# VectorE's first column sum for a pair of combined weights is queued behind the third remainder of the pair in front

## The chip, the cores and the metric

One core of one Trainium2 chip runs the whole program. The metric is the device time of one execution in microseconds, smaller is better; the median of three executions is given, and one further execution was recorded by the profiler. PE is TensorE's matmul, PEld its weight load, DVE is VectorE, ACT is ScalarE, POOL is GpSimd, SP issues DMAs.

## The reference

One layer of a hybrid trunk on 2048 frames of width 1024, in float32:

```python
h = rmsnorm(x, norm_mix_w)
u_b, u_c, u_h, z, xbc, dt_raw = split(h @ w_in)          # 1024 x 5648
y_a = short_conv_mixer(u_b, u_c, u_h, short_conv_w)       # u_b * conv3(u_c * u_h)
y_b = ssd_mixer(z, xbc, dt_raw, ...)                      # conv4, chunked state-space scan, gate, group norm
x = x + concat(y_a, y_b) @ w_out                          # 2048 x 1024
h = rmsnorm(x, norm_mlp_w)
x = x + square(relu(h @ w_up)) @ w_down                   # 1024 x 4096 and back
return rmsnorm(x, final_norm_w)
```

## The kernel before

Each float32 operand of a large matmul is split into two float32r parts: a high part `hi` (a cast on ACT, line 100 for weights) and the remainder `lo = raw - hi` (a subtraction on DVE, line 101). A product is then three matmuls, hi·hi, hi·lo and lo·hi (lines 296 to 298).

The input projection, the up projection and the down projection multiply 2x2 blocks with seven block products instead of eight (class `Seven`). Frames are taken in halves of 1024, a half being two blocks of 512 columns. Weights come in pairs of raw tiles r0 and r1, up to 1024 columns each, with a left half a and a right half b. `combine` makes of them four weight tiles in the order in which the products use them: r0 itself, s12, s34 and the right half of r1. The sums are, by halves of their tiles: s12a = r1a + r1b (line 252, which I call the first column sum), s12b = s12a - r0a, s34a = r0a - r1a, s34b = r0b - s12b (line 229 all three). Each of the four is split by `split_w`, so that a pair of weights has four casts and four remainders; the third remainder is that of s34.

`chain` runs the seven products of a pair in the order b11, t1, t2, b21, t3, b22, t4 with the accumulators px, py, px, pw, px, py, px: the three further products on px and the one on py add to what stands in the bank already. So what t2 left in px has to be copied out before t3's first matmul, and what t3 left before t4's. In the projections and the down projection one product is twelve matmuls of 512 columns. While pair n is multiplied, `chain` asks the generator `ahead` for the weights of pair n + 1: the loads after b11, the first two splits after b21, the third after b22, the fourth after t4.

This is the order in which the program is written down. A scheduler then orders each engine's instructions by written priority and by when it reckons that their inputs and buffers are there, so that an instruction can be moved far ahead of the place where it is written. Each engine executes its own list in that order; an instruction whose wait has not ended holds everything behind it on its engine. `tc.issue_after(ins)` gives the instructions of its block an edge without a semaphore: the scheduler may not put them ahead of `ins` on the same engine.

Buffers: raw tiles `wraw` have three, hi and lo four each, the sums `s` two. With three raw tiles, r0 and r1 of pair n + 1 and r0 of pair n + 2 are held at once; r1 of pair n + 2 takes the buffer that r0 of pair n + 1 leaves when its remainder is done.

`combine` runs for the first half of the input projection (20 pairs), the first half of the up projection (16) and all of the down projection (33). In the second halves of the two projections the sums are read back from memory (`pairs`, lines 323 to 325; stored at lines 255 and 261), with no sum on DVE. t3's evictions are on DVE, at line 776 in the input projection, 926 in the up projection and 1109 in the down projection. The work of the norm for the next half (lines 396 to 417, `lx` and `nb`) and the casts and remainders of the next activations (lines 368 and 369) run beside the products.

Of the kernel before, what the change touches and what calls it, by code (L numbers as in the profile page):

```python
# [11 lines left out]
F32 = mybir.dt.float32  # L12
F32R = mybir.dt.float32r
AF = mybir.ActivationFunctionType
ALU = mybir.AluOpType
# [25 lines left out]
def trunk(ctx: ExitStack, tc: tile.TileContext, x, w_in, w_dt, w_out, w_up, w_down, cvec, hrow, out):  # L41
    nc = tc.nc
# [37 lines left out]
        out=tri, in_=tri, compare_op=ALU.is_ge, fill=0.0, base=0, pattern=[[1, P]], channel_multiplier=-1  # L80
# [7 lines left out]
    def wtile(w=1024):  # L88
        hi = wp.tile([P, 1024], F32R, tag="whi", name="whi", bufs=4)[:, 0:w]
        lo = wp.tile([P, 1024], F32R, tag="wlo", name="wlo", bufs=4)[:, 0:w]  # L90
        return hi, lo
# [6 lines left out]
    def split_w(raw, eng):  # L98
        hi, lo = wtile(raw.shape[-1])
        nc.scalar.copy(hi, raw)  # L100
        eng.tensor_tensor(out=lo, in0=raw, in1=hi.bitcast(F32), op=ALU.subtract)  # L101
        return hi, lo

    def split_src(src):
        k = src.shape[1]
        return [t.rearrange("p (k c) -> p k c", k=k) for t in split_w(load_w(src), nc.vector)]
# [104 lines left out]
    class Seven:  # L211
# [35 lines left out]
        def combine(self, r0, r1, kept=None):  # L247
            w = r0.shape[-1] // 2
            a, b = slice(0, w), slice(w, 2 * w)
            yield split_w(r0, nc.vector)  # L250
            s12 = self.sumtile("s12")[:, 0 : 2 * w]
            nc.vector.tensor_tensor(out=s12[:, a], in0=r1[:, a], in1=r1[:, b], op=ALU.add)
            self.sub(s12[:, b], s12[:, a], r0[:, a])
            if kept is not None:
                nc.sync.dma_start(kept[:, 0], s12)
            yield split_w(s12, nc.vector)
            s34 = self.sumtile("s34")[:, 0 : 2 * w]
            self.sub(s34[:, a], r0[:, a], r1[:, a])
            self.sub(s34[:, b], r0[:, b], s12[:, b])
            if kept is not None:  # L260
                nc.sync.dma_start(kept[:, 1], s34)
            yield split_w(s34, nc.vector)
            yield split_w(r1[:, b], nc.vector)

        def chain(self, groups, ws, ahead, evict, after):
# [1476 lines left out]
```

## Time and profile before

| | us |
|---|---|
| median of three executions (2623.39 to 2628.8) | 2623.73 |
| the profiled execution | 2627.32 |
| its span, first to last instruction | 2625.6 |
| PE busy in the span | 2601.6 |
| DVE busy | 1917.3 |
| ACT busy | 1468.0 |

The profiled execution is 3.6 us longer than the median of the three, and its time holds 1.7 us around the span. Granted TensorE clock: 0.997 of full speed. Stages in the span: the start up to 85 us, first half of the input projection to 470, its second half with the first half of the scan to 940, output projection with the rest of the scan to 1372, up projection first half to 1655 and second half to 1985, down projection to 2590, tail.

How to read the lines: the timeline gives start, duration, engine, source line, operation, tiles, shape, count, and in brackets the idle time of the engine before the instruction with what ended it. A list of waits gives who waited for whom: total us, times, longest.

### The profile page before, as it was taken

The numbers are of one execution on the slowest core, as the hardware profiler recorded it, in microseconds if no ns is written. First come the engines' busy times: TensorE is split into PE (matmuls) and PEld (weight loads), VectorE is DVE, ScalarE is ACT, GpSimd is POOL, SyncE is SP. The second block draws the span as 40 slices with busy tenths as digits, with TensorE's granted clock in tenths as the row PEclk, the third lists the DMA queues.
The fourth block names the chain that finished last, engine by engine and source line by source line (L and its number), as shares of the span: only waits on it lengthen the run. The fifth ranks groups of instructions, "written<-read, shape, count | busy, mean of one in ns | idle before, by whom it ended". The sixth has DMA issues, their size and how long they took to land.

```text
span 2625.6 us, 33818 instructions
## 1 busy us (share of the span) xinstructions
PE 2601.6 (99%) x12139; PEld 2141.9 (82%) x12139; DVE 1917.3 (73%) x2631; ACT 1468.0 (56%) x2230; POOL 58.1 (2%) x99
## 2 busy tenths in 40 slices
PE   9999999999999999999999999999999999999998
PEld 7788888788888888888888888888888888888887
DVE  7877877777778777778677775744448887888985
ACT  7654345776667666768335555755556444444533
POOL 1010000000000000000000000000000000000001
PEclk9999999999999999999999999999999999999998
DMA  4545745644555578877656786765557654665762
GB/s 155 194 172 181 278 143 194 208 156 164 170 165 173 167 270 257 272 221 230 206 196 237 263 314 235 280 212 193 197 192 254 194 174 153 217 200 180 244 201 69
DMA packets 252169, 536.98 MB, mean 205 GB/s; under 512 B 26208, under 2 KB 93024, under 8 KB 252000
## 3 DMA queue, kind: packets, MB, share of 16 engines
q1 hardware_dynamic: 251856, 534.29, 61.1%
q8 instruction: 95, 1.56, 0.2%
q14 instruction: 74, 0.61, 0.1%
q10 hardware_dynamic: 144, 0.52, 0.1%
HBM read 354.89 MB, written 179.83 MB: 204 GB/s over the span
## 4 chain that ended last, share of the span: by engine, by line
PE 86%; DMA 5%; DVE 4%; ACT 3%; issue 2%; SPq 0%; POOL 0%; POOLq 0%; DVEq 0%; ACTq 0%
PE px L296 13%; PE px L297 13%; PE px L298 13%; PE py L296 6%; PE py L298 6%; PE py L297 6%; PE pm L113 4%; PE pm L114 4%; PE pm L115 4%; PE pw L296 3%; PE pw L298 3%; PE pw L297 3%; PE yd L1391 1%; PE yo L1388 1%; DMA ry<-yn_d 1%
## 5 line engine op out<-in xcount | busy, mean ns | idle before, releaser
L296 PE MATMUL px<-uh,whi 128*128 128x512 f32 x1672 | 655.7, 392 | 6.7 <-DVE res L1109 1.9
L298 PE MATMUL px<-uh,wlo 128*128 128x512 f32 x1672 | 651.4, 390 | 0.0
L297 PE MATMUL px<-ul,whi 128*128 128x512 f32 x1672 | 650.9, 389 | 0.0
L296 PEld LDWEIGHTS px<-uh,whi 128*128 128x128 f32 x1672 | 313.9, 188 | 80.8 <-DVE acc L1109 3.1
L101 DVE TENSOR_TENSOR wlo<-wraw,whi 128x512 fp32r<-128x512 f32 (+1 forms) x213 | 221.1, 1038 | 211.9 <-ACT whi L100 209.7
L298 PEld LDWEIGHTS px<-uh,wlo 128*128 128x128 f32 x1672 | 313.8, 188 | 66.0 <-issue 0.2
L297 PEld LDWEIGHTS px<-ul,whi 128*128 128x128 f32 x1672 | 314.0, 188 | 64.0
L100 ACT CAST whi<-wraw 128x1024 fp32r<-128x1024 f32 x214 | 193.9, 906 | 305.4 <-PE px L297 228.0
L100 ACT CAST whi<-s 128x1024 fp32r<-128x1024 f32 x210 | 219.9, 1047 | 228.4 <-PE py L297 95.0
L296 PE MATMUL py<-uh,whi 128*128 128x512 f32 x836 | 327.2, 391 | 1.3 <-ACT s L773 0.8
L298 PE MATMUL py<-uh,wlo 128*128 128x512 f32 x836 | 325.5, 389 | 0.0
L297 PE MATMUL py<-ul,whi 128*128 128x512 f32 x836 | 325.5, 389 | 0.0
L101 DVE TENSOR_TENSOR wlo<-s,whi 128x1024 fp32r<-128x1024 f32 x210 | 255.1, 1215 | 71.5 <-ACT whi L100 69.4
L113 PE MATMUL pm<-uh,whi 128*128 128x512 f32 (+1 forms) x648 | 251.6, 389 | 0.1
L114 PE MATMUL pm<-ul,whi 128*128 128x512 f32 (+1 forms) x648 | 248.2, 383 | 0.5 <-DVE ul L226 0.5
L115 PE MATMUL pm<-uh,wlo 128*128 128x512 f32 (+1 forms) x648 | 248.2, 383 | 0.0
L296 PEld LDWEIGHTS py<-uh,whi 128*128 128x128 f32 x836 | 156.9, 188 | 35.9 <-ACT s L773 1.3
L298 PEld LDWEIGHTS py<-uh,wlo 128*128 128x128 f32 x836 | 156.9, 188 | 32.7
L297 PEld LDWEIGHTS py<-ul,whi 128*128 128x128 f32 x836 | 157.0, 188 | 32.1
L368 ACT CAST uh<-rh 128x1024 fp32r<-128x1024 f32 (+1 forms) x128 | 120.4, 944 | 78.0 <-PE py L298 61.7
L296 PE MATMUL pw<-uh,whi 128*128 128x512 f32 x418 | 163.4, 391 | 0.0
L298 PE MATMUL pw<-uh,wlo 128*128 128x512 f32 x418 | 162.8, 389 | 0.0
(259 smaller groups left out, 3799.8 us busy)
## 6 DMA issues: line engine op xcount, KB each, us to landing
hid_d<-e SPq DMA_DIRECT2D x96, 512.0 KB, 3.9
rh<-hid_d SPq DMA_DIRECT2D x96, 512.0 KB, 4.3
wraw<-w_in SPq DMA_DIRECT2D x68, 512.0 KB, 3.9
wraw<-w_down SPq DMA_DIRECT2D x104, 256.0 KB, 3.7
wraw<-w_up SPq DMA_DIRECT2D x48, 512.0 KB, 4.1
dec<-rd_d SPq DMA_DIRECT2D x32, 512.0 KB, 5.7
wraw<-w_out SPq DMA_DIRECT2D x32, 512.0 KB, 5.0
x_d<-xt SPq DMA_DIRECT2D x64, 256.0 KB, 3.9
```

The costliest lines, as they stand in the source:

```text
L100: nc.scalar.copy(hi, raw)
L101: eng.tensor_tensor(out=lo, in0=raw, in1=hi.bitcast(F32), op=ALU.subtract)
L113: nc.tensor.matmul(out, whi, hi, start=(k == 0), stop=False)
L114: nc.tensor.matmul(out, whi, lo, start=False, stop=False)
L115: nc.tensor.matmul(out, wlo, hi, start=False, stop=(k == nk - 1))
L296: nc.tensor.matmul(p, hi, h[0], start=not seeded and k == 0, stop=False, **kw)
L297: nc.tensor.matmul(p, hi, h[1], start=False, stop=False, **kw)
L298: nc.tensor.matmul(p, lo, h[0], start=False, stop=(k == len(g) - 1), **kw)
L368: nc.scalar.copy(p[i][0], t)
L1388: nc.tensor.matmul(yo[:, j * L : (j + 1) * L], state[:, j * P : (j + 1) * P], cT, start=True, stop=True)
L1391: nc.tensor.matmul(yd[(i % 2) * 64 : (i % 2) * 64 + 64, (i // 2) * L : (i // 2 + 1) * L], byhead(t["xdt"])[:, i, :], t["dec"][:, i % 2 * 4 ...
```

## The change

From its second call on, `combine` writes its first column sum under `issue_after` of the third remainder of the pair whose weights were combined before. No instruction is added or removed.

```diff
     def split_w(raw, eng):
         hi, lo = wtile(raw.shape[-1])
         nc.scalar.copy(hi, raw)
-        eng.tensor_tensor(out=lo, in0=raw, in1=hi.bitcast(F32), op=ALU.subtract)
+        split["last"] = eng.tensor_tensor(out=lo, in0=raw, in1=hi.bitcast(F32), op=ALU.subtract)
         return hi, lo
+
+    split = {}
...
             s12 = self.sumtile("s12")[:, 0 : 2 * w]
-            nc.vector.tensor_tensor(out=s12[:, a], in0=r1[:, a], in1=r1[:, b], op=ALU.add)
+            cut = split.get("third")
+            with tc.issue_after(cut.ins) if cut else nullcontext():
+                nc.vector.tensor_tensor(out=s12[:, a], in0=r1[:, a], in1=r1[:, b], op=ALU.add)
...
-            yield split_w(s34, nc.vector)
+            parts = split_w(s34, nc.vector)
+            split["third"] = split["last"]
+            yield parts
             yield split_w(r1[:, b], nc.vector)
```

The order of instructions on DVE at two places. In these rows `s` is a tile of sums with its number, `wraw` a raw weight, `whi` and `wlo` its parts; line 252 of before is line 256 after, 229 is 231, 1109 is 1115, 369 is 375, 184 is 186, 776 is 782, 750 is 756.

A step of the down projection (at 2350 to 2361 us of the span), DVE before:

```order
L101 TENSOR_TENSOR wlo<-wraw,whi 128x1024
L369 TENSOR_TENSOR ul_19901<-rh,uh_19900 128x1024
L1109 TENSOR_TENSOR res<-pw,res 128x512
L101 TENSOR_TENSOR wlo<-s_19893,whi 128x1024
L252 TENSOR_TENSOR s_20039<-wraw 128x512
L1109 TENSOR_TENSOR res<-px,res 128x512
L229 TENSOR_TENSOR s_20039<-s_20039,wraw 128x512
L369 TENSOR_TENSOR ul_19940<-rh,uh_19939 128x1024
L1109 TENSOR_TENSOR acc<-py,acc 128x512
L101 TENSOR_TENSOR wlo<-s_19932,whi 128x1024
L369 TENSOR_TENSOR ul_19963<-rh,uh_19962 128x512
L229 TENSOR_TENSOR s_20078<-wraw 128x512
```

The same place after:

```order
L101 TENSOR_TENSOR wlo<-wraw,whi 128x1024
L375 TENSOR_TENSOR ul_19901<-rh,uh_19900 128x1024
L1115 TENSOR_TENSOR res<-pw,res 128x512
L101 TENSOR_TENSOR wlo<-s_19893,whi 128x1024
L1115 TENSOR_TENSOR res<-px,res 128x512
L375 TENSOR_TENSOR ul_19940<-rh,uh_19939 128x1024
L1115 TENSOR_TENSOR acc<-py,acc 128x512
L101 TENSOR_TENSOR wlo<-s_19932,whi 128x1024
L375 TENSOR_TENSOR ul_19963<-rh,uh_19962 128x512
L256 TENSOR_TENSOR s_20039<-wraw 128x512
L1115 TENSOR_TENSOR acc<-px,acc 128x512
L101 TENSOR_TENSOR wlo<-wraw,whi 128x512
```

The sum of the pair after the next (s_20039) stood ahead of t3's eviction `res<-px`; it now stands behind the third remainder (of s_19932), ahead of t4's eviction. Its three followers of line 229 come behind the fourth remainder.

A pair of the first half of the input projection (at 220 to 232 us), DVE before:

```order
L101 TENSOR_TENSOR wlo<-s_1925,whi 128x1024
L252 TENSOR_TENSOR s_2071<-wraw 128x512
L184 RECIPROCAL facc<-facc 128x512
L776 TENSOR_TENSOR eb<-px,s_1892 128x512
L776 TENSOR_TENSOR ea<-py,s_1906 128x512
L750 TENSOR_TENSOR eb<-eb,cc 128x512
L750 TENSOR_TENSOR ea<-ea,cc 128x512
L101 TENSOR_TENSOR wlo<-s_1967,whi 128x1024
L750 TENSOR_TENSOR eb<-px,cc 128x512
```

and after:

```order
L101 TENSOR_TENSOR wlo<-s_1925,whi 128x1024
L186 RECIPROCAL facc<-facc 128x512
L782 TENSOR_TENSOR eb<-px,s_1892 128x512
L782 TENSOR_TENSOR ea<-py,s_1906 128x512
L756 TENSOR_TENSOR eb<-eb,cc 128x512
L756 TENSOR_TENSOR ea<-ea,cc 128x512
L101 TENSOR_TENSOR wlo<-s_1967,whi 128x1024
L256 TENSOR_TENSOR s_2071<-wraw 128x512
L756 TENSOR_TENSOR eb<-px,cc 128x512
```

The sum left the place ahead of the norm's reciprocal and of t3's eviction `eb<-px`, and stands right ahead of t4's.

The scheduler's order of other engines moved too, in a few places. On ACT, at the second pair of the up projection (1393 to 1401 us), before:

```order
L929 ACTIVATE e_12162<-px 128x512
L100 CAST whi<-wraw 128x512
L930 ACTIVATE e_12162<-e_12162 128x512
L396 ACTIVATE lx<-lx 128x1024
L923 COPY s_12334<-px 128x512
L923 COPY s_12358<-py 128x512
L100 CAST whi<-wraw 128x1024
```

and after:

```order
L935 ACTIVATE e_12162<-px 128x512
L100 CAST whi<-wraw 128x512
L936 ACTIVATE e_12162<-e_12162 128x512
L929 COPY s_12334<-px 128x512
L929 COPY s_12358<-py 128x512
L100 CAST whi<-wraw 128x1024
```

The square of a loaded tile of the norm (`lx`) left the place ahead of the copies that empty px and py; it now stands one pair later. Its load on SP, which was issued between the stores of the two sums, now comes behind the next two weight loads.

## The prediction

> **What bounds the kernel now.** I read the page's busy times first, then busy times by stage, then who waits for what on DVE, then the timeline around each place where PE paused.
>
> ```profile
> PE 2601.6 (99%) x12139; PEld 2141.9 (82%) x12139; DVE 1917.3 (73%) x2631; ACT 1468.0 (56%) x2230; POOL 58.1 (2%) x99
> ```
>
> PE has 24.0 us of idle time in a span of 2625.6. Only that, and what a matmul that starts late loses besides, is there to win. By stage (columns: length, then busy us of PE, PEld, DVE, ACT, POOL, clock, DMA share, GB/s):
>
> ```profile
> 85.00:470.00 385.00, 382.95 (x1687) 315.42 (x1686) 292.58 (x352) 184.97 (x232) 25.49 (x40) 1.00 0.55 194
> 1372.00:1655.00 283.00, 281.98 (x1243) 232.85 (x1242) 193.32 (x256) 156.09 (x230) 0.00 (x0) 1.00 0.72 258
> 1655.00:1985.00 330.00, 330.00 (x1457) 272.92 (x1456) 169.35 (x199) 193.62 (x283) 0.00 (x0) 1.00 0.62 218
> 1985.00:2590.00 605.00, 601.97 (x2644) 494.68 (x2643) 491.81 (x630) 271.10 (x329) 0.00 (x0) 1.00 0.59 190
> ```
>
> The first, second and fourth rows are the stages that make sums on DVE; PE idles 2.05 + 1.02 + 3.03 = 6.1 us in them. In the third, the second half of the up projection, the sums are read back, and by its row PE does not idle at all: the same products without the sums run without a pause. So the sums, or what stands around them, are a suspect. On DVE:
>
> ```profile
> DVE s L252 <- DMA wraw<-w_down: 26.5, 19, 3.6
> ...
> DVE s L252 <- DMA wraw<-w_in: 11.4, 13, 1.8
> ...
> DVE s L252 <- DMA wraw<-w_up: 9.7, 9, 2.4
> ```
>
> The first column sum (line 252) waits for the load of r1 in 41 of its 69 executions, 47.6 us in all. DVE is not the bound, so this is harmless in itself. It hurts where t3's eviction stands behind it: t4's matmuls go to the same bank, and only b22's twelve matmuls, 12 x 0.23 = 2.7 us (the pitch is read below), cover that eviction.
>
> **The change, part by part.** The edit moves 68 of the 69 sums (the first has no pair in front); two of these, the first of the up and of the down projection, have a third remainder far in front and stay. The other 66 go behind it, past t3's eviction and mostly b22's. With each go the difference s12b of line 229, the store of s12 on SP in the 36 pairs that store it, and in part the two sums of s34. No duration changes. So the sum consists of pauses of PE.
>
> *First term, the worst step of the down projection:*
>
> ```profile
> 2351.14 2.33 SPq L1010 DMA_DIRECT2D wraw<-w_down  x2
> ...
> 2356.53 0.39 PE L297 MATMUL py<-ul,whi 128*128 128x512 f32 x1
> ...
> 2356.63 0.69 DVE L252 TENSOR_TENSOR s<-wraw 128x512 f32<-128x512 f32 x1 [2.65 <-DMA wraw<-w_down]
> 2356.76 0.39 PE L298 MATMUL py<-uh,wlo 128*128 128x512 f32 x1
> ...
> 2357.24 0.68 DVE L1109 TENSOR_TENSOR res<-px,res 128x512 f32<-128x512 f32 x1
> ...
> 2357.97 0.50 PE L296 MATMUL px<-uh,whi 128*128 128x512 f32 x1 [0.83 <-DVE res L1109]
> ```
>
> PE's matmuls follow each other by 0.23 us (2356.53 to 2356.76). The next starts 1.21 after its predecessor, 0.98 late, and takes 0.50 instead of 0.39, which delays its successor by another 0.11: 1.1 us. It waited for t3's eviction, whose input was there when b22 began, twelve matmuls before 2357.0, at 2354.3, and which stood behind the sum. With the sum gone DVE, idle for 2.65 us here, evicts at once and is done by 2355.0, 2 us before t4. All 1.1 us go. Two more of the kind:
>
> ```profile
> 2183.53 0.69 DVE L252 TENSOR_TENSOR s<-wraw 128x512 f32<-128x512 f32 x1 [2.29 <-DMA wraw<-w_down]
> ...
> 2184.02 0.39 PE L298 MATMUL py<-uh,wlo 128*128 128x512 f32 x1
> 2184.88 0.50 PE L296 MATMUL px<-uh,whi 128*128 128x512 f32 x1 [0.47 <-DVE acc L1109]
> ...
> 2414.75 0.69 DVE L252 TENSOR_TENSOR s<-wraw 128x512 f32<-128x512 f32 x1 [2.20 <-DMA wraw<-w_down]
> ...
> 2415.33 0.39 PE L298 MATMUL py<-uh,wlo 128*128 128x512 f32 x1
> 2416.09 0.50 PE L296 MATMUL px<-uh,whi 128*128 128x512 f32 x1 [0.38 <-DVE acc L1109]
> ```
>
> 0.86 - 0.23 + 0.11 = 0.75, and 0.76 - 0.23 + 0.11 = 0.65. Down projection: 1.1 + 0.75 + 0.65 = 2.5 us.
>
> *Second term, the input projection:*
>
> ```profile
> 222.14 0.69 ACT L183 ACTIVATE facc<-pss,cv 128x512 f32<-128x512 f32 x1
> ...
> 223.85 0.69 DVE L252 TENSOR_TENSOR s<-wraw 128x512 f32<-128x512 f32 x1 [1.76 <-DMA wraw<-w_in]
> 224.46 3.34 DVE L184 RECIPROCAL facc<-facc 128x512 f32<-128x512 f32 x1
> ...
> 227.08 0.39 PE L296 MATMUL px<-uh,whi 128*128 128x512 f32 x1
> 227.72 0.63 DVE L776 TENSOR_TENSOR eb<-px,s 128x512 f32<-128x512 f32 x1
> ...
> 228.40 0.50 PE L296 MATMUL px<-uh,whi 128*128 128x512 f32 x1 [0.93 <-DVE eb L776]
> ```
>
> The sum holds up the reciprocal, and this the eviction. PE loses 1.32 - 0.23 + 0.11 = 1.2 us. Without it the reciprocal starts when its input is there, 222.83, ends its turn 3.26 later (224.46 to 227.72), and the eviction ends at 222.83 + 3.26 + 0.63 = 226.7, ahead of 227.3. I count 1.1, since the new order of PE comes to that product two matmuls earlier.
>
> *Third term, the up projection.* Here the gain is not the sum's own:
>
> ```profile
> 1396.21 0.63 ACT L930 ACTIVATE e<-e 128x512 f32<-128x512 f32 x1
> 1398.46 1.06 ACT L396 ACTIVATE lx<-lx 128x1024 f32<-128x1024 f32 x1 [1.62 <-DMA lx<-x_d]
> ...
> 1398.71 0.39 PE L298 MATMUL pw<-uh,wlo 128*128 128x512 f32 x1
> ...
> 1399.42 0.57 ACT L923 COPY s<-px 128x512 f32<-128x512 f32 x1
> ...
> 1400.04 0.50 PE L296 MATMUL px<-uh,whi 128*128 128x512 f32 x1 [0.94 <-ACT s L923]
> ```
>
> ACT's copy of px stands behind a square that waits for a load; PE loses 1.33 - 0.23 + 0.11 = 1.2. In the new order the copy follows the instruction of 1396.21 and ends near 1397.4. The square goes one pair on, its load behind weight loads. If it waited there as long, it would cost up to 1.2 again; I take nothing, since it then stands behind the third cast, some 10 us later.
>
> *What stays or is added.* The sum with its 0.69 now stands ahead of t4's eviction or the fourth remainder; it waits there only if r1 has not landed. Four pairs of the input projection get the next pair's first cast ahead of the second SiLU and of the copy of px after t2:
>
> ```profile
> 333.04 1.06 ACT L734 ACTIVATE cacc<-cacc 128x1024 f32<-128x1024 f32 x1 [1.46 <-DVE cacc L731]
> 333.05 0.39 PE L296 MATMUL pw<-uh,whi 128*128 128x512 f32 x1
> ...
> 334.00 0.57 ACT L773 COPY s<-px 128x512 f32<-128x512 f32 x1
> 334.47 1.05 ACT L100 CAST whi<-wraw 128x1024 fp32r<-128x1024 f32 x1
> ...
> 335.77 0.39 PE L296 MATMUL px<-uh,whi 128*128 128x512 f32 x1
> ```
>
> The cast can start when t2 has ended, 333.05; then cast, SiLU and copy take 0.95 + 0.96 + 0.57 (starts to starts, the copy whole) and end at 335.5, while t3 starts at 335.77. They fit by 0.2 to 0.3 us, so 0 us; late by that, each of the four costs 0.1 to 1.2. The stores of s12 go later on SP, behind up to two weight loads; their readers are a half away, so nothing.
>
> Sum: 2.5 + 1.1 + 1.2 = 4.8 us. I give back 0.1 for the tight places: 4.7. In the profiled execution, 2627.32, that is 2622.6; its 3.6 us over the median I take to stay out of it, so 2623.73 - 4.7 = 2619.0, or -0.18%. A measurement of this kernel tells about 0.2%, 5.2 us, from no change.
>
> **The rivals.**
>
> *More goes than the named pauses* (2614.5 to 2618). Idle time in the three stages is 6.1 us by the rows, and each pause costs some 0.27 more than its idle row says (1.1 against 0.83). With a dozen pauses that is 6.1 + 12 x 0.27 = 9.3, the floor at 2614.4. For it: shorter pauses of the same kind exist. Against: part of them belong to the casts of the next activations, which stay. Some 6.5 us, 2617.
>
> *The wait only moves.* The load of r1 still starts only when r0's remainder has left the buffer:
>
> ```profile
> DMA to landing us min/median/max: 3.1/4.2/8.2
> ```
>
> In the step at 2356 the sum's new place comes after the third remainder, about 3 us after the landing seen. If the loads take near 8.2 there, DVE waits again, now ahead of t4's eviction, and half of the gain is lost: 2621.4. With the median landing it does not. The Trainium skill, "Perfetto Trace Analysis", section "Optimization Strategy", says that a bubble that repeats can mean that there is not enough SBUF for the next tile; by that rule a fourth raw tile would be the cure and a new order would not, and the time would stay at 2623.7. The rows agree that the buffer sets the load's start, not that the sum must be where it was.
>
> *The tight casts* on ACT miss in all four pairs at 1.2 each: 4.7 - 4.7, 2623.7. It decides from a conv chain on DVE 0.3 us late.
>
> *t4's eviction is late, slower.* In the pairs of the input projection whose t4 DVE evicts, twelve, the bank is needed by the next pair's t1:
>
> ```profile
> 363.79 0.69 DVE L229 TENSOR_TENSOR s<-wraw 128x512 f32<-128x512 f32 x1
> ...
> 364.40 0.68 DVE L750 TENSOR_TENSOR ch<-px,cc 128x512 f32<-128x512 f32 x1
> ...
> 365.69 0.39 PE L296 MATMUL py<-uh,whi 128*128 128x512 f32 x1
> ```
>
> The eviction ends at 365.08, 0.6 ahead of need, with one sum of 0.61 ahead of it already. Where the moved sum comes on top, up to 0.61 + 0.11 are added to PE: 12 x 0.72 = 8.6, net 3.9 slower, 2627.6; with a wait in the sum more. It decides when the third remainder ends 0.6 us later than here. Against: this pair's remainder was itself delayed by the waiting sum.
>
> **How the numbers follow.** The forecast, 2618.0 to 2619.9, 0.57, of which a third lies beyond 5.2 us; more goes 0.17; the wait moves 0.11; tight casts 0.10; late eviction 0.05, half of it over 2629 with a wait in the sum. Faster by over 0.2%: 0.17 + 0.2 = 0.37. Slower: 0.03. Within: 0.60. The range leaves out the lowest tail of the second case and the last two in part: 2615.2 to 2623.6.
>
> **What would show it.** Right: the waits of line 256 for loads fall from 47.6 us to under 10; PE's pauses at 228, 1400, 2184, 2357 and 2416 are gone; PE idles under 3 us in the three stages. Wrong: PE waits for `ch` or `eb` of line 756 at the start of a py product, for `s` of line 779 (the copy of px) in the conv pairs, or the load wait stands at line 256 as before. The prediction fails if the pauses of this one profile are not those of most executions.

## The result and the profile after

The changed kernel takes 2618.51 us (median of nine executions, 2615.68 to 2620.42) against 2623.73 of nine of the kernel before: ratio 0.9976, 95% interval 0.9967 to 0.9984, that is -5.2 us. Two later comparisons, on two chips, gave 0.9977 (0.9969 to 0.9986) and 0.9984 (0.9975 to 0.9993). All three intervals lie below 1, and the gain, about 0.2%, is about the least that a measurement of this kernel can tell. The profiled execution took 2618.51 us, its span 2616.6; the one of before had 2625.6, so the two traces differ by 9.0 us, more than the medians do.

The page's busy times, and busy times by stage (length, then PE, PEld, DVE, ACT, POOL, clock, DMA share, GB/s):

```profile
PE 2597.3 (99%) x12139; PEld 2142.4 (82%) x12139; DVE 1916.0 (73%) x2631; ACT 1468.1 (56%) x2230; POOL 61.2 (2%) x99
```

```profile
85.00:470.00 385.00, 383.39 (x1689) 315.91 (x1688) 292.12 (x352) 184.94 (x233) 29.57 (x40) 1.00 0.54 195
1372.00:1655.00 283.00, 283.00 (x1250) 234.43 (x1249) 191.92 (x256) 155.94 (x231) 0.00 (x0) 1.00 0.72 259
1655.00:1985.00 330.00, 329.83 (x1454) 272.23 (x1453) 171.34 (x201) 194.56 (x284) 0.00 (x0) 1.00 0.63 220
1985.00:2590.00 605.00, 603.19 (x2682) 498.75 (x2681) 492.65 (x632) 271.04 (x331) 0.00 (x0) 1.00 0.59 188
```

No engine does other work than before. PE's idle time falls from 24.0 to 19.3 us, in the three stages with sums on DVE from 6.1 to 1.61 + 0 + 1.81 = 3.4; in the up projection's first half it is zero. The moved instruction by itself (its line, and what DVE waited for ahead of it):

```profile
L256 DVE TENSOR_TENSOR s<-wraw x69: 421/684/693, 31.9 to 2529.3; 128x512 f32<-128x512 f32 x68, 128x256 f32<-128x256 f32 x1
its engine sat idle before it (us, times) until:
  DMA wraw<-w_down: 0.8, 1
```

47.6 us of waits in 41 sums have become 0.8 in one: at its new place r1 has landed. The step of the down projection that was the worst, in the timeline:

```profile
2349.79 0.69 DVE L1115 TENSOR_TENSOR res<-px,res 128x512 f32<-128x512 f32 x1 [0.48 <-PE px L304]
...
2352.08 0.39 PE L304 MATMUL py<-uh,wlo 128*128 128x512 f32 x1
2352.31 0.39 PE L302 MATMUL px<-uh,whi 128*128 128x512 f32 x1
...
2355.16 0.68 DVE L256 TENSOR_TENSOR s<-wraw 128x512 f32<-128x512 f32 x1
2355.76 0.68 DVE L1115 TENSOR_TENSOR acc<-px,acc 128x512 f32<-128x512 f32 x1
```

t3's eviction runs as soon as t3 ends and is done 1.8 us ahead of t4's first matmul, which follows its predecessor at the usual 0.23. The sum comes 5.4 us after that eviction, and t4's eviction is held up by nothing but the sum's 0.6 us. The pair of the input projection:

```profile
223.36 3.35 DVE L186 RECIPROCAL facc<-facc 128x512 f32<-128x512 f32 x1 [0.78 <-ACT facc L185]
...
226.63 0.63 DVE L782 TENSOR_TENSOR eb<-px,s 128x512 f32<-128x512 f32 x1
...
227.12 0.39 PE L303 MATMUL px<-ul,whi 128*128 128x512 f32 x1
...
227.35 0.46 PE L302 MATMUL px<-uh,whi 128*128 128x512 f32 x1
```

Here almost nothing is left over: the eviction ends at 227.26 and PE starts at 227.35, on time. And ACT in the up projection, where the copy of px now follows at once:

```profile
1393.85 0.63 ACT L936 ACTIVATE e<-e 128x512 f32<-128x512 f32 x1
1394.38 0.57 ACT L929 COPY s<-px 128x512 f32<-128x512 f32 x1
```

Two places are new. Once, at 288.7, the rival with the late eviction of t4 did occur:

```profile
287.85 0.68 DVE L256 TENSOR_TENSOR s<-wraw 128x512 f32<-128x512 f32 x1
...
288.45 0.68 DVE L756 TENSOR_TENSOR ch<-px,cc 128x512 f32<-128x512 f32 x1
...
289.28 0.47 PE L302 MATMUL py<-uh,whi 128*128 128x512 f32 x1 [0.19 <-DVE ch L756]
```

It cost 0.35 + 0.08 us, in this profile alone of the seven that I have with that order of the input projection. And late in the down projection DVE waits for a cast of ACT, and ACT for a load of `rh`, ahead of an eviction, this time of t2:

```profile
2515.50 1.05 ACT L374 CAST uh<-rh 128x1024 fp32r<-128x1024 f32 x1 [3.52 <-DMA rh<-hid_d]
...
2516.58 1.23 DVE L375 TENSOR_TENSOR ul<-rh,uh 128x1024 fp32r<-128x1024 f32 x1 [2.03 <-ACT uh L374]
...
2518.33 0.68 DVE L231 TENSOR_TENSOR s<-s,wraw 128x512 f32<-128x512 f32 x1
2518.93 0.69 DVE L231 TENSOR_TENSOR s<-wraw 128x512 f32<-128x512 f32 x1
2519.53 0.68 DVE L231 TENSOR_TENSOR s<-wraw,s 128x512 f32<-128x512 f32 x1
2520.13 0.68 DVE L1115 TENSOR_TENSOR acc<-px,acc 128x512 f32<-128x512 f32 x1
...
2520.87 0.50 PE L302 MATMUL px<-uh,whi 128*128 128x512 f32 x1 [1.34 <-DVE acc L1115]
```

The three sums of line 231 are the moved sum's followers; they take 1.8 us between the remainder and the eviction. Before, only two of them stood there, and PE did not pause at this place; it had paused for 1.3 us a step earlier, at 2512.

**A measure for the stages.** To compare many profiles I add up, in each stretch, by how much matmuls of 512 columns start later than 0.227 us after their predecessor, where that is more than 0.025 (late matmuls, in us). It takes in idle time and the slower first matmul behind a pause. The whole execution has 34.1 us of it before and 27.0 after; the 85 us at the start have about 6 of it in every profile.

### The profile page after: what moved, and what is told of

The parts are those of the page before. It is cut to its first block, busy times and chain, and to the rows that moved or that the text cites. A ratio compares the mean times of both kernels' runs of the same rounds, so it can differ in the third digit from the quotient of the medians.

```text
span 2616.6 us, 33846 instructions
## 1 busy us (share of the span) xinstructions
PE 2597.3 (99%) x12139; PEld 2142.4 (82%) x12139; DVE 1916.0 (73%) x2631; ACT 1468.1 (56%) x2230; POOL 61.2 (2%) x99
## 3 DMA queue, kind: packets, MB, share of 16 engines
q8 instruction: 95, 1.56, 0.2%
## 4 chain that ended last, share of the span: by engine, by line
PE 89%; DMA 4%; DVE 3%; ACT 2%; issue 2%; POOL 0%; SPq 0%; POOLq 0%; DVEq 0%; ACTq 0%
PE px L302 14%; PE px L304 14%; PE px L303 14%; PE py L302 7%; PE py L303 7%; PE py L304 7%; PE pm L115 4%; PE pm L116 4%; PE pm L117 4%; PE pw L302 3%; PE pw L304 3%; PE pw L303 3%; PE yd L1397 1%; PE yo L1394 1%; PE pd L669 1%
## 5 line engine op out<-in xcount | busy, mean ns | idle before, releaser
L375 DVE TENSOR_TENSOR ul<-rh,uh 128x1024 fp32r<-128x1024 f32 (+1 forms) x128 | 138.6, 1087 | 34.0 <-ACT uh L374 34.0
```

Of the source, the lines that this page charges most:

```text
L375: nc.vector.tensor_tensor(out=p[i][1], in0=t, in1=p[i][0].bitcast(F32), op=ALU.subtract)
```

## The experiments

**One stage at a time.** The same edge, but given only where the condition holds (`kept` is None in the down projection alone; `Proj` is the input projection, `Mlp` the up projection):

```diff
-            cut = split.get("third")
+            cut = split.get("third") if kept is None else None                                   # e1
+            cut = split.get("third") if kept is not None and isinstance(self, Proj) else None    # e2
+            cut = split.get("third") if kept is not None and isinstance(self, Mlp) else None     # e3
```

> The edge stands only in the down projection (32 of its 33 sums); input and up projection keep the order of before. My theory, that the place ahead of t3's eviction costs PE a pause per late load: -2.5 us of the -5.2, that is about 2621 us beside 2623.7, and PE's pauses near 2184, 2357 and 2416 gone while those near 228 and 1400 stay. Rival one, that the two profiles' difference by stage is the truth (PE's late matmuls lost 5.0 us in this stage before and 2.4 after): -2.7, which cannot be told from the first by time alone. Rival two, that the whole gain comes from this stage, the only one with 19 waits and 26.5 us: -5. Rival three, that the wait only moved and the gain came from elsewhere: 0.

> The edge stands only in the first half of the input projection. My theory: the one pause near 228 goes, -1.1 us, about 2622.6; the tight casts on ACT cost nothing. Rival: the difference of the two profiles there, 3.3 to 2.7 us of late matmuls, since t4's eviction was once late at 288.7 and a SiLU at 461.6 later than before: -0.6. Rival, that a place ahead of t4's eviction harms: 0 or slower by up to 2.

> The edge stands only in the first half of the up projection. My theory: -1.2 us at the square of the loaded tile that leaves its place ahead of ACT's copies at 1400, and the pause of 0.24 + 0.11 at 1506, where DVE waits: -1.2 to -1.6, about 2622.3. PE idles 0 in this stage, as in the profile after. Rival: the pause at 1400 is one execution's, and returns at the square's new place one pair later: 0.

Measured against 2625.82 of before on that chip: down 2621.8, ratio 0.9984 (0.9976 to 0.9993); input 2624.6, 0.9993 (0.9984 to 1.0001); up 2626.36, 0.9995 (0.9986 to 1.0005). Only the down projection is distinguishable from nothing in time. The order of the other stages stayed that of before, so these profiles, too, say whether the pauses that I read from one execution belong to most. Each pause was there in every profile with the old order at its place, with its own size each time, and in none with the new (late start and slow first matmul together, us; the old orders are those of the kernel before, e1 to e3 and, further down, e5, as far as they leave the place alone):

| place | old order | new order |
|---|---|---|
| 228 | 1.2, 0.79, 0.77, 0.89 | 0.07 or less |
| 1400 | 1.21, 1.02, 1.51 | 0 |
| 2184 | 0.75, 0.81, 1.12, 1.26 | 0 |
| 2357 | 1.1, 0.71, 0.87, 0.74 | 0 |
| 2416 | 0.65, 0.52, 0.70, 1.7 | 0 |

e3 missed its expectation in time: 1.2 to 1.6 us less were expected, and its median is 0.5 us above that of before, although its stage had no late matmul. The pause at 1506 that this expectation counts is less sure than the five: 0.35 us in the kernel before, 0.30 in e1, none in e2, all with the old order there.

**Only behind t3's eviction.** The sum gets its edge to t3's eviction of the products in front, not to the third remainder:

```diff
-            cut = split.get("third")
+            cut = split.get("t3")
...
-                        nc.vector.tensor_tensor(out=t, in0=pm[p], in1=t, op=ALU.add)
+                        split[name] = nc.vector.tensor_tensor(out=t, in0=pm[p], in1=t, op=ALU.add)
```

(the evictions of the two projections alike).

> The sum is queued only behind t3's eviction of the products in front, not behind the third remainder: 30-odd sums move by one or two instructions, the order of ACT stays that of before, and in the third stage the square stays ahead of the copies. My theory, that only the place ahead of t3's eviction costs: the sum still waits for its load (20 to 45 us of DVE waits at the sum's line remain of 47.6), yet the pauses of input and down projection go: -3.6 us, about 2620.1; the pause near 1400 stays, 1.2 us. Rival one, that the wait itself has to go, wherever it stands, since it holds up the remainders and b22's eviction behind it: at most half of that, -1 to -2. Rival two, that the later place behind the third remainder brings something of its own: time between the two kernels but pauses at 2184, 2357 and 2416 gone all the same.

2621.44, ratio 0.9979 (0.9969 to 0.9989), -4.4 us by the medians, the size of the whole change. What DVE still waited for ahead of the sum:

```profile
  DMA wraw<-w_down: 9.2, 12
  DMA wraw<-w_in: 6.3, 6
  DMA wraw<-w_up: 1.8, 2
```

and the step whose sum stood ahead of t3's eviction at 2414 in the kernel before:

```profile
2407.60 0.69 DVE L1113 TENSOR_TENSOR acc<-px,acc 128x512 f32<-128x512 f32 x1 [0.48 <-PE px L302]
2410.42 0.69 DVE L256 TENSOR_TENSOR s<-wraw 128x512 f32<-128x512 f32 x1 [2.13 <-DMA wraw<-w_down]
```

The sum waits as long as it did in the kernel before, 2.13 us beside 2.20, but t3's eviction is done before it, and PE loses nothing there. In all, 17.3 us of waits remain in 20 sums (fewer than I expected), and the pauses at 228, 2184, 2357 and 2416 are gone all the same. What costs is the eviction behind the waiting instruction, not the wait. One small pause, 0.13 + 0.11 us at 2280, stayed: there b22's and t4's evictions stand behind the sum, and only five of b22's matmuls cover t4's. The pause near 1400 is there with 0.71 + 0.11, as ACT's order did not move.

**The square alone.** The kernel before, with one square of the norm behind the copies:

```diff
+                        behind = anchor and (bb, k) == (1, 4)
-                        nc.scalar.activation(t, t, AF.Square)
+                        with tc.issue_after(anchor[0].ins) if behind else nullcontext():
+                            nc.scalar.activation(t, t, AF.Square)
...
-                nc.scalar.copy(s[name], pm)
+                ins = nc.scalar.copy(s[name], pm)
+                if (h, q, name) == (0, 1, "s5"):
+                    anchor.append(ins)
```

> No sum is moved: the kernel before, in which only one square of the norm's loaded tiles in the first half of the up projection is queued on ACT behind the two copies that it stood ahead of. My theory, that the third term is this square's and not the sums': PE's pause near 1400 (0.7 to 1.4 us late in the four profiles with the old order, 0 in the two with the new) is gone, those near 228, 1506, 2184, 2357 and 2416 stay; -1.2 us, about what the interval can tell, so the profile decides. Rival, that the moved sum itself freed ACT's copy: the pause stays and the time is that of before.

```profile
1395.41 0.58 ACT L927 COPY s<-px 128x512 f32<-128x512 f32 x1
1396.88 0.59 ACT L927 COPY s<-py 128x512 f32<-128x512 f32 x1 [0.90 <-PE py L300]
1397.36 1.06 ACT L400 ACTIVATE lx<-lx 128x1024 f32<-128x1024 f32 x1
```

No sum was moved, DVE waits 7.2 us at the sums of the up projection, and the stage has no late matmul at all: 0.00 against 1.56. (The scheduler also put three matmuls of pw behind those of px, so that px was needed 0.7 us sooner, not later.) The small pause at 1506 is not there either, but as it is also missing in e2, this says nothing of its cause. The time did not show it: 2624.47 against 2624.47, ratio 0.9995 (0.9986 to 1.0004). At 1683, where ACT's copy stands behind casts of the first activations of the second half, 0.42 + 0.11 us were lost.

**The sum on another engine.** The kernel before, with `nc.gpsimd.tensor_tensor` for the first column sum.

> The order is not touched by hand: the first column sum is issued on GpSimd instead of VectorE, so that the wait for r1's load is on an engine that has nothing else to do. An addition of this shape took 1.30 us there against 0.69 on VectorE. My theory, that it costs only because t3's eviction stands behind it: the pauses near 228, 2184, 2357 and 2416 go, -3 to -5 us, less what the scheduler's other order brings. Rival, that the two engines hinder each other: VectorE's busy time rises by more than the sums' 47 us that left it fall, and the time does not improve.

Slower: 2640.45, ratio 1.0054 (1.0042 to 1.0067). Both theories missed what the waits of DVE (us in total, times, longest) and the timeline show:

```profile
DVE s L229 <- POOL s L252: 78.1, 47, 3.7
```

```profile
2287.55 0.69 DVE L229 TENSOR_TENSOR s<-s,wraw 128x512 f32<-128x512 f32 x1 [2.19 <-POOL s L252]
2288.16 0.68 DVE L1109 TENSOR_TENSOR acc<-py,acc 128x512 f32<-128x512 f32 x1
2288.76 1.22 DVE L369 TENSOR_TENSOR ul<-rh,uh 128x1024 fp32r<-128x1024 f32 x1
2289.89 0.68 DVE L1109 TENSOR_TENSOR acc<-py,acc 128x512 f32<-128x512 f32 x1
...
2291.62 1.28 DVE L1109 TENSOR_TENSOR acc<-px,acc 128x512 f32<-128x512 f32 x2
2292.36 0.50 PE L296 MATMUL px<-uh,whi 128*128 128x512 f32 x1 [1.79 <-DVE acc L1109]
```

The wait for the load left DVE, and the second sum, s12b, now waits there for the first, with evictions behind it: 78.1 us in place of 47.6, and PE stands idle for 1.79 us up to 2292.36. The order of much else changed too, so not all of the 16 us is shown to be this. The price of the other engine itself is 1.29 us per sum (the median; 0.69 on VectorE), and VectorE's other instructions took 0.9% longer (1917.3 - 47.2 = 1870.1 us before, 1887.6 here). The Trainium skill, "Perfetto Trace Analysis", section "Optimizing Scalar/DVE Operations", warns that moving work between these two may not help because they share a port; the 0.9% is the most that this run shows of that.

**The changed kernel again, and later loads.** e8 and e10 are the changed kernel itself. e7 writes the next activations' casts and remainders in `refill` one product later; e9 does it in the down projection only.

```diff
-            i = {"t1": 0, "b21": 1, "b22": 2, "t4": 3}.get(name)
+            i = {"t2": 0, "t3": 1, "b22": 2, "t4": 3}.get(name)
...
-            i = {"b11": 0, "t1": 1, "b21": 2, "b22": 3}.get(name)
+            i = {"b11": 0, "t2": 1, "t3": 2, "b22": 3}.get(name)
```

> The changed kernel, and the casts and remainders of the next activations in the down projection are written one product later (behind t2 and t3 instead of t1 and b21), their loads too. In the profile after, the one pause of weight left in that stage, 1.5 + 0.1 us at 2519, is a remainder that waits for such a load ahead of t2's eviction; the kernel with the edge in the down projection alone had 0.27 and 0.23 at those places. If that load is the next cause: -1 us against the changed kernel, 2.4 us of late matmuls in the stage fall under 1.3. Rival: the remainders then stand ahead of t3's or b22's evictions and the pause only moves: 0 to +1.

> The changed kernel itself, beside the others on one chip. By the three stages apart: -4 (down), -1.2 (input) and -1.3 (up) of their medians or ratios make -6.5; by my terms -4.7; the first comparison gave -5.2, with 2.2 us on either side. The pauses near 228, 1400, 2184, 2357 and 2416 must be gone again, whatever stands at 288 and 2519.

> The changed kernel with the one part of the run before that paid: inside the down projection the next activations' casts and remainders come one product later; at the end of the up projection, where the run before got a new pause of 3.0 us at 1987, they stay where they were. If that pause was what ate the gain: late matmuls in the down projection 1.1 to 1.3 us (2.4 and 2.5 in the two profiles of the changed kernel), those at 1987 gone, and -1 to -1.2 us against the changed kernel, about 0.9973 of the time before. Rival, that it is noise of loads: 2 to 2.5 us in the stage again, and the time of the changed kernel.

> The changed kernel once more, as the yardstick of the run beside it: -5.2 to -6 us by the two comparisons so far (0.9976 and 0.9977). The named pauses stay gone; at 1681, where the second half of the up projection takes its first loaded activations, 0.1 us were lost in one profile and 2.1 in the other: if that is the gain of the first half being given back at a load, 0 to 2 are to be seen there again.

e8 is 2618.73 against 2624.47, e10 2617.75 against 2621.79. e7 is 2622.52 (0.9994, 0.9985 to 1.0003), no gain left: 1.2 us of late matmuls in the down projection (2000 to 2590), as hoped, but a new pause of 3.0 us that begins at 1987. That looked as if the down projection's part were worth keeping, and e9 refuted it: 2616.91 (0.9981, 0.9972 to 0.999), the same as e10, and 3.1 us late in the stage. e7 and e9 have the same order there, so 1.2 and 3.1 differ by their executions and not by an edit. e8 also shows one place where the up projection's gain may go, at the first loads of its second half:

```profile
1680.90 0.39 PE L304 MATMUL py<-uh,wlo 128*128 128x512 f32 x1
...
1681.63 1.04 ACT L374 CAST uh<-rb 128x1024 fp32r<-128x1024 f32 x1 [1.06 <-DMA rb<-hn_d]
1682.58 0.58 ACT L309 COPY pw<-px 128x512 f32<-128x512 f32 x1
...
1683.21 0.50 PE L302 MATMUL px<-uh,whi 128*128 128x512 f32 x1 [1.92 <-ACT pw L309]
```

ACT waits for the load of the activations, ahead of the copy that PE needs. If PE comes earlier and the load does not, the gain is lost here. But 2.1 us were lost here in e8, 0.1 in the first profile after, nothing in e10, and 0.56 in e2, which has the old order of the up projection and had won nothing. So these runs do not show that the gain is given back here.

**The same cure elsewhere.** What is left in the down projection has the same form; in e10, DVE:

```profile
2498.97 0.75 DVE L1254 SCALAR_TENSOR_TENSOR lf<-lf,cv,facc 128x512 f32<-128x512 f32 x1 [2.79 <-DMA lf<-fin_d]
2499.63 0.69 DVE L231 TENSOR_TENSOR s<-s,wraw 128x512 f32<-128x512 f32 x1
2500.24 0.68 DVE L1115 TENSOR_TENSOR acc<-px,acc 128x512 f32<-128x512 f32 x1
```

So the changed kernel, with the last norm's multiplications a product after their loads and behind the latest eviction of px:

```diff
                     t = load(d)
+                    yield
                     for i in range(2):
-                        nc.vector.scalar_tensor_tensor(
+                        with tc.issue_after(split["px"].ins):
+                            nc.vector.scalar_tensor_tensor(
```

> The changed kernel, in which the other instruction of the down projection that waits for a load ahead of an eviction is treated the same way: the last norm's multiplications of loaded tiles lf are written one product after their loads, behind the latest eviction of px. In the changed kernel they stood ahead of evictions of px at five places, and by its profiles 0.5 to 1.8 us are lost at 2440 to 2520 behind a wait for lf or rh. If the rule carries over: late matmuls from 2430 to 2590 fall from 1.3 to 1.9 us to 0.7 or less, -0.6 to -1.2 against the changed kernel, about 2617.5; too small for the time alone. Rival, that other loads take their place (rh's cast ahead of t2's eviction at 2519): 1.3 to 2 us remain there.

2616.37 against 2621.99, ratio 0.9976 (0.9967 to 0.9985), the lowest median of all, though its interval takes in the ratio of e10 on the same chip, 0.9984. Late matmuls from 2430 to 2590 are 0.69, and DVE waits for no lf at all (3.5 us in e10):

```profile
2439.29 0.69 DVE L1115 TENSOR_TENSOR acc<-px,acc 128x512 f32<-128x512 f32 x1 [1.85 <-PE px L304]
2439.90 1.41 DVE L1258 SCALAR_TENSOR_TENSOR lf<-lf,cv,facc 128x512 f32<-128x512 f32 x2
```

One value of 0.69 means little, since e1 and e2 had 0.71 and 0.70 there without this edit. That the waits for lf are gone is shown; that the time is lower is not.

## Why the prediction was right, and where it was off

Late matmuls in us, in four profiles with the old order at the place and four with the new, in three stretches with what follows them. Old: the kernel before and, as far as they leave the stage alone, e1, e2, e3, e5. New: the changed kernel, e8, e10, and the one of e1 to e3 that changes the stage. (For the up projection three old ones, since e5 changes it.)

| stretch | old order | new order | mean difference |
|---|---|---|---|
| input 85 to 450 | 1.64, 1.04, 1.13, 1.61 | 0.76, 0.33, 0.33, 0.33 | -0.9 |
| its end and the scan's start, to 520 | 3.96, 4.53, 5.23, 4.84 | 3.42, 3.80, 5.10, 5.04 | -0.3 |
| up 1372 to 1640 | 1.56, 1.32, 1.51 | 0.00, 0.03, 0.00, 0.00 | -1.45 |
| up, second half, to 1980 | 0.24, 0.26, 0.89 | 0.44, 2.43, 0.24, 1.17 | +0.6 |
| down 2020 to 2430 | 3.48, 3.52, 4.09, 4.68 | 0.44, 0.44, 0.44, 0.44 | -3.5 |
| down, to 2590 | 1.40, 0.70, 1.82, 1.12 | 1.79, 1.90, 1.27, 0.71 | +0.2 |

They add up to -5.4 us, beside -5.2, -5.7 and -4.0 by the medians of the three comparisons. So the accounts agree within their scatter, and the time, 2618.5 against 2619.0 forecast, came out by the named mechanism. That it came so near is partly luck: the first term was 1.0 us too small, and what the rows behind the three stages add or take is not told from noise.

- *The mechanism, a waiting sum ahead of t3's eviction*: right. The waits fell to 0.8 us (I had asked for under 10), the five pauses went. e4 sharpens it: the wait may stay if the eviction is in front. Its late matmuls in the three stretches of the first, third and fifth row were 0.33, 0.81 (the pause near 1400) and 0.68.
- *First term, down projection, 2.5 us*: mis-sized, 3.5. I summed the three pauses that were long in one profile. The short ones there, 0.23 at 2108, 0.19 at 2396 and others of the kind, make 3.48 - 0.44 = 3.0 in that very profile, and in other executions the same places wait longer (0.5 to 1.7 at 2416), or one at 2282 besides. The rival "more goes" was right that far.
- *Second term, input projection, 1.1*: 0.9 there, 1.2 with what follows. Right, but by a thinner margin than the 0.6 us worked out: the eviction ended 0.09 us ahead of need. PE comes to that product two matmuls (0.45 us) earlier in the new order; the prediction names this, but takes it off the gain and not off the margin.
- *Third term, up projection, 1.2*: right in cause, as e5's profile shows without any moved sum. The pause near 1400 was 1.25 on the average of the three old profiles; the rest of the 1.45 is the pause at 1506, whose cause is open. So about a quarter of the gain comes from ACT's order, which the scheduler changed, and not from the waits of DVE.
- *Given back, 0.1*: open. The tight casts on ACT, for which I took it off, cost nothing that the input row shows, and the row behind the up projection has +0.6; but that mean rests on 2.43 in e8 and 1.17 in e3, other profiles with the new order there had 0.24 to 0.54, and one with the old order 0.89. The +0.2 at the end of the down projection is mainly the net of two: the pause at 2512 (1.30, 0, 0.88 and 1.01 with the old order) is gone, and the one at 2519 (1.61, 0.82, 0.08 and 0.34 with the new order, none with the old) has come. I had not foreseen it.
- *The 3.6 us of the profiled execution over the median*: rightly kept out. From 520 to 1372, which the change does not touch, the profiles have 12.2 to 14.9 us of late matmuls, 14.9 in the one of before and 12.5 in the one after: 2.4 of the 9.0 us between the two traces.
- *The rivals*: the wait did not move to the new place (0.6 to 0.8 us in the three profiles of the changed kernel). The casts in the conv pairs kept their time. t4's eviction was late once, 0.43 us, not twelve times. The Trainium skill ("Perfetto Trace Analysis", section "Optimization Strategy") says that a repeated bubble can mean too little memory for the next tile. What the prediction drew from it, that a new order would then not help, did not come true: the waits went with the same three raw tiles. Whether a fourth raw tile would do as much was not tried.
- *PE idles under 3 us in the three stages*: 3.4, missed. 1.34 of it is the pause at 2519: another load, with the moved sum's three followers ahead of the eviction.

## What to carry to other kernels

Look not for the longest wait of an engine but for what stands behind it in the queue: 47.6 us of waits on VectorE cost PE about 4.4 (0.9 in the input and 3.5 in the down projection), where an eviction with 2.7 us of cover or less came next, and queueing the waiting instruction behind that eviction won nearly all of it while part of the wait remained. Read the other engines' order too: a quarter of this gain came from an instruction of ACT that the scheduler moved along. Moving the waiting instruction to an idle engine did not help here, where its follower stayed in the queue. Count a pause by several executions. Look also at the stage behind, where a load that nothing brings forward may take back what was won; these runs suggest that and do not settle it.

## What the runs showed of the hardware

At the places read here the landing of loads makes executions differ. With the same instructions in the same order, the sum near 2414 waited 2.06, 2.20, 2.24 and 3.22 us for its load (e2, before, e3, e5), and the pause behind it was 0.52, 0.65, 0.70 and 1.7 us. From 2020 to 2430 with the new order, where no sum that waits for its load stands ahead of t3's eviction, all four profiles had 0.44 us of late matmuls. An addition of 128x512 took 1.29 us on GpSimd (median, in e6) and 0.69 on VectorE.
